# Alternating delta-rule pairs and state-space groups in the scan part of a hybrid decoder block

## The chip, the core and the metric

The kernel runs on one core of one Trainium2 chip. The metric is the device time of one execution in microseconds (us). The engines are TensorE (PE for products, PEld for the loads of the stationary operand), VectorE (DVE), ScalarE (ACT), GpSimd (POOL) and SyncE (SP), whose queue issues every DMA here. Each engine works its own list of instructions in order; a semaphore wait at the head of a list holds up all that stands behind it.

## The reference, cut to what matters

One decoder block on 512 tokens of width 1024, all in float32. A normed and modulated input `h` is projected by one wide matrix; two token mixers work on the parts, their outputs are projected up, gated, merged, projected out, and a squared-ReLU MLP follows.

```python
h = rmsnorm(x, norm_mix_pre) * (1 + sc1) + sh1
proj = h @ w_in                       # z_ssm, xbc, dt, qkv, z_gdn, b, a, gate_ssm, gate_gdn
xbc = silu(causal_conv4(xbc) + b)     # state-space branch: 32 heads in 8 groups, chunks of 128
  y_diag = (C B^T * decay) x ;  y_off = C state * exp(acum)
  state  = state * exp(a_last) + B^T (w_s x)
qkv = silu(causal_conv4(qkv))         # delta-rule branch: 16 value heads, 8 key/query heads
  (I + a_low) [u, w] = [v b, k b e^g]          # unit triangular solve
  v_new = u - w state ;  o = q e^g state + attn v_new
  state = state * exp(g_last) + k_dec^T v_new
merged = sigmoid(gate_ssm) * (y_ssm @ w_ssm_up) + sigmoid(gate_gdn) * (y_gdn @ w_gdn_up)
x = x + g1 * rmsnorm(merged @ w_out) ;  x = x + g2 * rmsnorm(relu(h2 @ w_mlp_up)**2 @ w_mlp_down)
```

## The kernel before, in words

Every dense product of two float32 matrices is made of three products of rounded parts (`mm3`, lines 147 to 150: high by high, low by high, high by low). Weights come in blocks of 128 by 1024 (`raw`), are split by ACT (high part) and DVE (low part), and three blocks of each kind are in flight. A block of 128 output channels costs 24 products of 512 columns.

The program has five stages. The **front** (0 to about 60 us of the trace) loads the tokens, builds the modulation and transposes `h` into `hT`. The **scan part** (to about 915 us) makes the dense products of `w_in` and runs the two mixers under them. Then come the **up-projections**, the **output projection**, and the **MLP**.

The scan part works on 16 items: items 0 to 7 are pairs of delta-rule heads (one key/query head, two value heads), items 8 to 15 are state-space groups of four heads. For each item there are:

- `dense_in(i)` (line 556): four blocks of channels, each followed by a four-tap convolution and Silu (`conv`). It writes the item's keys and queries into a ring of buffers `kq`.
- `dense_z(i)` (line 587): the gate z, products of 256 columns.
- a preparation, `gdn_prep` or `ssd_prep`. Both load a decay matrix by DMA (`decay`, line 690, tiles `dec` or `dc`; ACT then applies eight Relu pieces, line 697, and one Exp). `gdn_prep` forms the triangular matrix `bt` (line 768) from key products (PE, line 762) and starts `solve`.
- `solve` (line 799), delta-rule items alone: `bt` goes out to DRAM and back as `Nb` (line 808) so that all 32x32 blocks lie one row to a partition; 31 steps of two POOL operations (lines 817 and 819) invert them; the result goes to DRAM and back into a tile `U` (line 830).
- a scan. `gdn_scan` (line 834) widens the inverses from 32 to 128 (PE lines 850, 860, 863, 874, 882, with ACT writing `Z1` and `Z2` and DVE writing `T6` and `U` between), then runs the recurrence over four chunks: PE 897 (state by keys and queries), DVE 902, PE 918 (by `U`), DVE 923, PE 931 (state update), DVE 938. `ssd_scan` (line 1079) does the like with PE 1090, 1108 and 1111; POOL adds the skip term (line 1128).
- an end: norm, gate z, transposes (PE 998 or 1164) and a store of `y` to DRAM (`put_y`, line 704).

Eight further blocks of `w_in` (the branches' gates, `("g", g)`) are fillers inside the scan part; the other eight are made behind it (`proj_ch`, line 1225 on), where PE would otherwise wait for the reload of `y`.

The order of all this is not written out. `Weave` (line 33) is a planner that runs while the program is built: each piece of work is a generator that issues some instructions and yields an estimate of their duration (`PE(..)`, `A(n)`, `V(n)`, `G(n)`, or `("S", t)` for a latency such as a DMA), or a list with a mark to wait for. The planner keeps a clock per engine and always issues next the first stream in rank whose last result is expected by now. The dense stream has the last rank, so dense products fill the places where the planner thinks that no scan step is ready. The estimates thus set each engine's order of instructions, and nothing else; on the chip each instruction waits for its true operands. Rings such as `kq`, `dec`, `zs` limit how far a stream runs ahead; `pb` is a ring of three PSUM banks for the scan steps.

In the kernel before, the order of items is 0, 1, ..., 15: first all delta-rule pairs, then all state-space groups (`heads`, line 1171).

Of the kernel before, what the change touches and what calls it, by code (L numbers as in the profile page):

```python
# [10 lines left out]
F32 = mybir.dt.float32  # L11
# [103 lines left out]
def hybrid_block(ctx: ExitStack, tc: tile.TileContext, x, cols, drow, rows, w_ada, w_ch, w_z,  # L115
# [86 lines left out]
    NG = 8  # L202
# [6 lines left out]
    acap = {"bt": (3, 1), "zs": (3, 1), "kq": (3, 3), "vt": (2, 2), "dec": (4, 4)}  # L209
# [18 lines left out]
    def loads():  # L228
        """The first transfers, in the order of their use."""
# [147 lines left out]
    def early_ch(n):  # L377
# [3 lines left out]
        for k in range(KD):  # L381
# [3 lines left out]
            yield PE(0.64)  # L385
# [22 lines left out]
    Us = [sp.tile([P, 8, P], F32, name=f"U{i}", bufs=1) for i in range(2)]  # L408
# [8 lines left out]
    def chan_of(i):  # L417
        """Blocks of w_ch of a head pair or group, in the order of their use."""
# [5 lines left out]
    # the order of the dense products: heads' and groups' channels, their gates z, the branches' gates as fillers  # L424
    seq = [("in", 0), ("g", 0), ("g", 1), ("g", 2), ("in", 1), ("z", 0), ("in", 2), ("z", 1)]
    seq += [("g", g) for g in range(3, NG)]
    for i in range(3, 16):
        seq += [("in", i), ("z", i - 1)]
    seq.append(("z", 15))
    plan, adas = [], list(range(16))  # L430
    for kind, i in seq:
        blocks = [b for b in chan_of(i)] if kind == "in" else [64 + i] if kind == "g" else []
        plan += [("w", ("c", b), w_ch[1 + b]) for b in blocks if 1 + b not in early + later]
        if kind == "z":
            plan += [("w", ("z", i, h), w_z[2 * i + h]) for h in range(2)]
            for _ in range(2 if i > 14 else i > 0):
# [99 lines left out]
    def dense_ch(blk):  # L536
# [50 lines left out]
    def dense_z(i):  # L587
        if i > 2:
            yield [("end", i - 3)]
# [5 lines left out]
        for tp in range(2):  # L595
            bk, ps = yield from bank("ps")
            for th in range(2):
                ts = slice((2 * tp + th) * P, (2 * tp + th + 1) * P)
                for k in range(KD):
# [114 lines left out]
    def gdn_prep(hq):  # L714
# [12 lines left out]
        for j in range(2):  # L727
# [71 lines left out]
    def solve(hq, btu):  # L799
        """Inverses of the unit triangular 32x32 diagonal blocks: every fourth row of one on a partition."""  # L800
# [4 lines left out]
        yield ("S", 4.0)  # L805
# [7 lines left out]
        yield ("S", 4.0)  # L813
# [17 lines left out]
        yield ("S", 4.0)  # L831
        wv.mark(("U", hq))

    def gdn_scan(hq):
        if hq:
            yield [("scan", hq - 1)]
# [3 lines left out]
        U = Us[hq % 2]  # L840
# [6 lines left out]
        Z1 = sp.tile([P, 8, 32], F32, tag="Z1", name="Z1", bufs=1)  # L847
# [24 lines left out]
        Z2 = sp.tile([P, 8, 64], F32, tag="Z2", name="Z2", bufs=1)  # L872
# [15 lines left out]
        # the recurrence over chunks  # L888
# [62 lines left out]
    def gdn_out(hq, c, dec, kd, u2, o, qs, so, ku2, kqs):  # L951
# [17 lines left out]
        yield A(P, 2)  # L969
# [261 lines left out]
    # up-projections, gated merge  # L1231
# [32 lines left out]
    # output projection, residual, norm of the MLP's input  # L1264
# [254 lines left out]
```

## Time and profile before

| | |
|---|---|
| device time, median of 3 runs | 1552.59 us (1549.88 to 1553.95) |
| span of the profiled execution | 1540.2 us; its own device time is not listed |
| PE busy | 1488.7 us, 97% of the span |
| PEld, DVE, ACT, POOL busy | 1271.8, 879.4, 741.4, 373.7 us |
| mean granted TensorE clock | 0.977 of full speed |

The busy time of PE counts each product until its modelled end, and products overlap, so 97% hides a good deal: a product at half the clock is busy for longer. Reading it by stretches, with the granted clock beside it, tells more than the sum. The span leaves out what lies ahead of the first and behind the last instruction; the median is 12.4 us above it. A PE instruction in the kernel's order is two passes in the trace where its operands are plain float32, so counts differ by that factor.

### The profile page before, as it was taken

The page shows a single profiled execution, that of the slowest core. Times are in us where ns is not written, and L with a number is a line of the kernel's source. Part 1 is how long each engine was busy: PE and PEld are TensorE (multiplying, and loading weights), DVE is VectorE, ACT ScalarE, POOL GpSimd, SP SyncE. Part 2 cuts the span into 40 slices and gives each one's busy share as a digit, 9 for nine tenths or more (in the row PEclk, how much of TensorE's full clock was granted, in tenths as well). Part 3 has the DMA queues.
Part 4 walks back from the last instruction along what each step waited for, and adds up shares of the span by engine and source line. Part 5 has one row for each costly group of instructions (what it writes and reads, how often), then busy time and mean ns, then how long its engine had stood idle before and what let it go on. Part 6 is the DMA issues. An engine that isn't in the chain of part 4 may idle for free.

```text
span 1540.2 us, 22637 instructions
## 1 busy us (share of the span) xinstructions
PE 1488.7 (97%) x8520; PEld 1271.8 (83%) x8520; DVE 879.4 (57%) x1564; ACT 741.4 (48%) x1393; POOL 373.7 (24%) x715
## 2 busy tenths in 40 slices
PE   7999898999999889999999999999999999999998
PEld 7788787888878679888888978888887888888886
DVE  5776456665757666866766764252377524344344
ACT  5585335453455275775667735242345433232232
POOL 6203455163363370333332230000002000000002
PEclk9999899997999989999999999999999999999999
DMA  7434443343524523344433459553363322222221
GB/s 279 151 119 114 127 105 91 101 136 100 127 76 128 140 80 114 134 128 144 135 122 129 142 169 304 190 192 109 123 212 110 110 96 96 96 96 96 96 96 69
DMA packets 87069, 199.45 MB, mean 129 GB/s; under 512 B 32504, under 2 KB 33024, under 8 KB 86960
## 3 DMA queue, kind: packets, MB, share of 16 engines
q1 hardware_dynamic: 86960, 198.01, 40.5%
q8 instruction: 67, 1.10, 0.3%
q14 instruction: 42, 0.34, 0.1%
HBM read 181.10 MB, written 16.88 MB: 129 GB/s over the span
## 4 chain that ended last, share of the span: by engine, by line
PE 81%; DMA 7%; POOL 4%; DVE 4%; issue 2%; ACT 2%; SPq 1%; POOLq 0%; ACTq 0%; DVEq 0%
PE ps L148 15%; PE ps L150 15%; PE ps L149 15%; PE pl L150 8%; PE pl L148 8%; PE pl L149 8%; DMA dec<-acd 2%; PE pb L1108 2%; DMA Nb<-btd 2%; POOL Ub L819 1%; DMA dc<-acd 1%; POOL tm L817 1%; PE pb L897 1%; PE pb L918 1%; PE pb L954 1%
## 5 line engine op out<-in xcount | busy, mean ns | idle before, releaser
L148 PE MATMUL ps<-hT,whi 128*128 128x512 f32 x688 | 291.6, 424 | 0.1
L150 PE MATMUL ps<-hT,whi 128*128 128x512 f32 x688 | 272.5, 396 | 0.0
L149 PE MATMUL ps<-hT,wlo 128*128 128x512 f32 x688 | 271.8, 395 | 0.0
L144 DVE TENSOR_TENSOR wlo<-raw,whi 128x1024 fp32r<-128x1024 f32 x119 | 146.7, 1233 | 217.3 <-ACT whi L143 215.3
L143 ACT CAST whi<-raw 128x1024 fp32r<-128x1024 f32 x119 | 124.7, 1048 | 229.5 <-PE pl L149 62.7
L148 PE MATMUL ps<-whi,hT 128*128 128x256 f32 (+1 forms) x536 | 165.3, 308 | 0.0
L463 DVE TENSOR_TENSOR wlo<-raw,whi 128x1024 fp32r<-128x1024 f32 x98 | 124.7, 1274 | 55.9 <-ACT whi L461 55.5
L150 PE MATMUL ps<-wlo,hT 128*128 128x256 f32 (+1 forms) x536 | 155.7, 291 | 0.0
L149 PE MATMUL ps<-whi,hT 128*128 128x256 f32 (+1 forms) x536 | 155.4, 290 | 0.0
L150 PEld LDWEIGHTS ps<-hT,whi 128*128 128x128 f32 x688 | 131.0, 190 | 29.0
L148 PEld LDWEIGHTS ps<-hT,whi 128*128 128x128 f32 x688 | 131.4, 191 | 26.2 <-issue 1.1
L149 PEld LDWEIGHTS ps<-hT,wlo 128*128 128x128 f32 x688 | 131.6, 191 | 23.9 <-issue 0.4
L525 DVE SCALAR_TENSOR_TENSOR cv<-ps,col,cv 128x511 f32<-128x511 f32 (+1 forms) x180 | 132.8, 741 | 16.1 <-ACT cv L519 13.4
L461 ACT CAST whi<-raw 128x1024 fp32r<-128x1024 f32 x98 | 102.2, 1043 | 64.6 <-PE ps L150 40.9
L817 POOL TENSOR_TENSOR tm<-Ub,Nb 128x60 f32<-128x60 f32 (+24 forms) x248 | 81.3, 328 | 135.3 <-DMA Nb<-btd 117.4
L148 PEld LDWEIGHTS ps<-whi,hT 128*128 128x128 f32 x536 | 103.8, 194 | 2.1 <-issue 0.4
L149 PEld LDWEIGHTS ps<-whi,hT 128*128 128x128 f32 x536 | 103.8, 194 | 1.6
L150 PEld LDWEIGHTS ps<-wlo,hT 128*128 128x128 f32 x536 | 103.5, 193 | 1.2 <-DVE wlo L144 0.3
L819 POOL TENSOR_TENSOR Ub<-Ub,tm 128x60 f32<-128x60 f32 (+24 forms) x248 | 84.8, 342 | 19.4
L1410 POOL TENSOR_TENSOR ya<-ya,gate 128x512 f32<-128x512 f32 x4 | 5.9, 1474 | 324.8 <-ACT junk L1408 324.8
L148 PE MATMUL pl<-hT,whi 128*128 128x512 f32 (+1 forms) x184 | 66.7, 364 | 1.0 <-DVE hT L190 1.0
L149 PE MATMUL pl<-hT,wlo 128*128 128x512 f32 (+1 forms) x184 | 66.2, 363 | 0.4 <-DVE wlo L144 0.4
(496 smaller groups left out, 3138.1 us busy)
## 6 DMA issues: line engine op xcount, KB each, us to landing
raw<-in_w_ch SPq DMA_DIRECT2D x81, 512.0 KB
raw<-in_w_ada SPq DMA_DIRECT2D x48, 512.0 KB
raw<-in_w_z SPq DMA_DIRECT2D x32, 512.0 KB
raw<-in_w_up SPq DMA_DIRECT2D x32, 512.0 KB
raw<-in_w_mu SPq DMA_DIRECT2D x32, 512.0 KB
raw<-in_w_md SPq DMA_DIRECT2D x32, 512.0 KB
ydr<-y SPq DMA_DIRECT2D x32, 256.0 KB
dc<-acd SPq DMA_DIRECT2D x16, 512.0 KB
```

What stands on the lines that cost most here:

```text
L143: sc.copy(hi, raw)
L144: ve.tensor_sub(out=lo, in0=raw, in1=hi.bitcast(F32))
L148: pe.matmul(ps, lhsT=lhs[0], rhs=rhs[0], start=first, stop=False)
L149: pe.matmul(ps, lhsT=lhs[1], rhs=rhs[0], start=False, stop=False)
L150: pe.matmul(ps, lhsT=lhs[0], rhs=rhs[1], start=False, stop=last)
L461: sc.copy(hi, raw)
L463: ve.tensor_sub(out=lo, in0=raw, in1=hi.bitcast(F32))
L525: ve.scalar_tensor_tensor(out=t[:, s:], in0=ps[:, :T - s], scalar=col[:, o + k:o + k + 1], in1=t[:, s:], op0=MUL, op1=ADD)
L817: gp.tensor_tensor(out=t3, in0=Ub[:, 0:r, j:j + 1].to_broadcast([P, r, n]), in1=Nb[:, j:j + 1, j + 1:32].to_broadcast([P, r, n]), op=MUL)
L819: gp.tensor_tensor(out=Ub[:, 0:r, j + 1:32], in0=Ub[:, 0:r, j + 1:32], in1=t3, op=SUB)
L897: pe.matmul(psk[:, j * 256:(j + 1) * 256], lhsT=kq[:, c, j, :], rhs=S, start=True, stop=True)
L1108: pe.matmul(psy[:, h * 64:(h + 1) * 64], lhsT=M[h // 2][:, h % 2, c, :], rhs=xd[:, c, h, :], start=True, stop=True)
```

## The change

Three things change in the scan part, and all of them act through the planner.

1. **Order of items.** `ORDER` mixes pairs and groups: 0, 8, 1, 2, 9, 3, 10, 4, 11, 5, 12, 6, 7, 13, 14, 15. Scans, preparations, ends and dense work all follow it. `before(i, n)` is the item n places ahead in it.
2. **Buffers and fillers.** The ring `kq` gets four buffers for three (an item's dense work may begin once the scan four places ahead is done). Room for it comes from one `U` for two (a pair's inverses are loaded into `U` once the scan of the pair before has ended) and from `Z1` and `Z2` sharing a buffer. Five more gate blocks become fillers (13 for 8): two after the second gate z, three and five near the end; three are left to `proj_ch`.
3. **Estimates.** The durations that the planner uses are changed: ACT 0.27 + n/1330 us, DVE 0.19 + n/975, POOL 0.24 + n/500, three dense products 0.68 us (0.36 for 256 columns), decay load 8.0 us (4.0 before), `bt` to DRAM 5.5 (4.0), `Nb` 10.0 (4.0), store of the inverses 5.0 (2.3), load of `U` 5.0 (4.0).

```diff
+ORDER = (0, 8, 1, 2, 9, 3, 10, 4, 11, 5, 12, 6, 7, 13, 14, 15)
+FILL = {2: 2, 15: 3, 16: 5}
 def A(n, k=1, f="A"):
-    return f, k * (0.25 + n / 1400)
+    return f, k * (0.27 + n / 1330)
...
-    NG = 8
+    NG = 3 + sum(FILL.values())
-    spare = (("kq", 3), ("vt", 2))
+    spare = (("kq", 4), ("vt", 2))
...
-    Us = [sp.tile([P, 8, P], F32, name=f"U{i}", bufs=1) for i in range(2)]
+    Us = [sp.tile([P, 8, P], F32, name=f"U{i}", bufs=1) for i in range(1)]
...
-    seq += [("g", g) for g in range(3, NG)]
-    for i in range(3, 16):
-        seq += [("in", i), ("z", i - 1)]
-    seq.append(("z", 15))
+    line = ORDER
+    at = {i: n for n, i in enumerate(line)}
+    def before(i, n):
+        return line[at[i] - n] if at[i] >= n else None
+    seq, fill = [("in", line[0]), ("g", 0), ("g", 1), ("g", 2)], list(range(3, NG))
+    for n in range(1, 17):
+        seq += [("in", line[n])] if n < 16 else []
+        seq.append(("z", line[n - 1]))
+        seq += [("g", fill.pop(0)) for _ in range(FILL.get(n, 0))]
...
     def dense_in(i):
-        if i > 2:
-            yield [("scan", i - 3)]
+        if at[i] > 3:
+            yield [("scan", before(i, 4))]
...
     def decay(i, hd, dst, key):
-        yield ("S", 4.0)
+        yield ("S", 8.0)
...
     def solve(hq, btu):
-        if hq > 1:
-            yield [("scan", hq - 2)]
-        U = Us[hq % 2]
+        if hq:
+            yield [("scan", hq - 1)]
+        U = Us[0]
...
     def heads(one, two):
-        for i in range(8):
-            yield from one(i)
-        for i in range(8):
-            yield from two(i)
+        for i in line:
+            yield from one(i) if i < 8 else two(i - 8)
```

Line numbers in the changed kernel are higher by 2 in the front and by 10 or 11 in the scan part (PE line 897 becomes 908, 918 becomes 929, 931 becomes 942, 762 becomes 773, 850 becomes 861; ACT line 697 becomes 708; POOL line 817 becomes 828). How the order of instructions moves is shown at three places.

**PE, recurrence of a pair.** Before, pair 4, from its second state update (`u3`, L931) to the next product by the state (L897):

```order
L931 MATMUL pb_4467<-u3_4436,kt_3116 128x256
L148 MATMUL ps_4473<-whi_4072,hT_96 128x256
L149 MATMUL ps_4473<-whi_4072,hT_97 128x256
L150 MATMUL ps_4473<-wlo_4073,hT_96 128x256
L731 MATMUL pa_4479<-ident_69,kq_3957 128x128 x4
L897 MATMUL pb_4484<-S_4469,kq_2828 128x256 x2
L954 MATMUL pb_4495<-u2_4438,dec_3085 128x128 x2
```

Now, pair 5, from its second state update (L942) to the first product of the group behind it (L1102, `xw`):

```order
L942 MATMUL pb_6992<-u3_6979,kt_5503 128x256
L150 MATMUL ps_6880<-whi_6690,hT_110 128x256
L151 MATMUL ps_6880<-whi_6690,hT_111 128x256
L152 MATMUL ps_6880<-wlo_6691,hT_110 128x256
L908 MATMUL pb_7008<-S_6994,kq_4972 128x256 x2
L965 MATMUL pb_7017<-u2_6981,dec_5500 128x128 x2
L929 MATMUL pb_7024<-r_7011,U0_125 128x128 x2
L942 MATMUL pb_7040<-u3_7027,kt_5503 128x256
L908 MATMUL pb_7053<-S_7042,kq_4972 128x256 x2
L965 MATMUL pb_7062<-u2_7029,dec_5500 128x128 x2
L929 MATMUL pb_7066<-r_7056,U0_125 128x128 x2
L1102 MATMUL pb_7074<-xw_6481,bt__6166 128x256
```

Before, dense products stand between the steps; in the changed order pair 5 (and likewise pair 3) runs its third chunk and the start of the fourth with none between.

**ACT, a decay load beside a pair's scan.** Before, pair 6 (`Z`, L877 is its last widening step; L697 are the Relu pieces on `dc` of group 0; L908 empties a bank of the recurrence):

```order
L877 ACTIVATE Z_5511<-pb 64x512
L529 ACTIVATE vT<-cv 128x512
L697 ACTIVATE dc<-dc,tok_114 128x128 x4
L519 ACTIVATE cv<-ps,col 128x512
L697 ACTIVATE dc<-dc,tok_114 128x128 x2
L1023 COPY bt__5579<-pa 128x512
L697 ACTIVATE dc<-dc,tok_114 128x128 x4
L908 ACTIVATE qs<-pb,tok_115 128x128 x2
```

Now, pair 1 with the `dc` of group 1 (L708 are the Relu pieces, L919 empties the bank):

```order
L888 ACTIVATE Z_2921<-pb 64x512
L708 ACTIVATE dc<-dc,tok_114 128x128 x12
L472 CAST whi<-raw 128x1024
L532 ACTIVATE cv<-ps,col 128x512
L708 ACTIVATE dc<-dc,tok_114 128x128 x2
L711 ACT_TABLE_LOAD
L711 ACTIVATE dc<-dc 128x1024
L540 ACT_TABLE_LOAD
L540 ACTIVATE kq<-cv 128x4x128
L919 ACTIVATE qs<-pb,tok_115 128x128 x2
```

In both, Relu pieces on a tile that comes by DMA stand ahead of a step of the running recurrence.

**POOL, a solve.** Before, the start of pair 3's solve (`Ub`, `tm`, `Nb`):

```order
L986 TENSOR_TENSOR ro<-so,mhalf 128x8
L812 COPY Ub<-eye 128x256
L817 TENSOR_TENSOR tm<-Ub,Nb 128x31
L819 TENSOR_TENSOR Ub<-Ub,tm 128x31
L817 TENSOR_TENSOR tm<-Ub,Nb 128x30
L819 TENSOR_TENSOR Ub<-Ub,tm 128x30
```

Now, the start of the same solve (L828, L830), with the skip terms (L1140) and gate products (L1160) of group 1:

```order
L823 COPY Ub<-eye 128x256
L1140 TENSOR_TENSOR t__3976<-t__3976,xk 128x256
L1140 TENSOR_TENSOR t__4002<-t__4002,xk 128x256
L1140 TENSOR_TENSOR t__4022<-t__4022,xk 128x256
L828 TENSOR_TENSOR tm<-Ub,Nb 128x31
L830 TENSOR_TENSOR Ub<-Ub,tm 128x31
L828 TENSOR_TENSOR tm<-Ub,Nb 128x30
L830 TENSOR_TENSOR Ub<-Ub,tm 128x30
L828 TENSOR_TENSOR tm<-Ub,Nb 128x29
L830 TENSOR_TENSOR Ub<-Ub,tm 128x29
L1160 TENSOR_TENSOR xk<-xk,zs 128x256
L828 TENSOR_TENSOR tm<-Ub,Nb 128x28
```

Operations of a group now stand between the steps of a pair's solve, where before there were none.

More of the change, by code (lines that the diff above doesn't have):

```diff
@@ L96, in A @@
 def A(n, k=1, f="A"):
-    return f, k * (0.25 + n / 1400)
+    return f, k * (0.27 + n / 1330)
 def V(n, k=1):
-    return "V", k * ((0.11 if n < D else 0.07) + n / 960)
+    return "V", k * (0.19 + n / 975)
 def G(n, k=1):
-    return "G", k * (0.15 + n / 500)
+    return "G", k * (0.24 + n / 500)
 def PE(t):
@@ L205, in hybrid_block @@
     POOLW = (1, 3, 5)
-    spare = (("kq", 3), ("vt", 2))
+    spare = (("kq", 4), ("vt", 2))
     wspare = ("bt", "zs", "o")
     ahalf = ("bt", "zs", "kq", "vt", "kq", "vt", "kq", "bt", "zs", "kq", "dec", "dec", "dec", "dec", "vt", "kq")
-    acap = {"bt": (3, 1), "zs": (3, 1), "kq": (3, 3), "vt": (2, 2), "dec": (4, 4)}
+    acap = {"bt": (3, 1), "zs": (3, 1), "kq": (4, 4), "vt": (2, 2), "dec": (4, 4)}
     akeys = {}
@@ L384, in early_ch @@
             mm3(ps, (w[0][:, ks], w[1][:, ks]), hT[k], k == 0, k == KD - 1)
-            yield PE(0.64)
+            yield PE(0.68)
         wv.mark(("early", n))
@@ L422, in chan_of @@
         return 48 + g, 56 + g, 32 + 2 * g, 33 + 2 * g
-    seq = [("in", 0), ("g", 0), ("g", 1), ("g", 2), ("in", 1), ("z", 0), ("in", 2), ("z", 1)]
-    seq += [("g", g) for g in range(3, NG)]
-    for i in range(3, 16):
-        seq += [("in", i), ("z", i - 1)]
-    seq.append(("z", 15))
+    line = ORDER
[7 more added lines that the diff above has]
+        seq += [("g", fill.pop(0)) for _ in range(FILL.get(n, 0))]
+    assert not fill
     plan, adas = [], list(range(16))
@@ L435, in hybrid_block @@
             plan += [("w", ("z", i, h), w_z[2 * i + h]) for h in range(2)]
-            for _ in range(2 if i > 14 else i > 0):
+            for _ in range(2 if at[i] > 14 else at[i] > 0):
                 plan += [("a", (adas[0], hf), w_ada[2 * (8 + adas[0]) + hf]) for hf in range(2)]
@@ L550, in dense_ch @@
             mm3(ps, (w[0][:, ks], w[1][:, ks]), hT[k], k == 0, k == KD - 1)
-            yield PE(0.64)
+            yield PE(0.68)
         if 1 + blk not in later:
@@ L556, in dense_in @@
     def dense_in(i):
-        if i > 2:
-            yield [("scan", i - 3)]
-        first = sp.tile([P, NC, 2, P] if i < 8 else [P, 2, NC, P], F32, tag="kq", name="kq", bufs=3)
+        if at[i] > 3:
+            yield [("scan", before(i, 4))]
+        first = sp.tile([P, NC, 2, P] if i < 8 else [P, 2, NC, P], F32, tag="kq", name="kq", bufs=4)
         pair = []
@@ L587, in dense_z @@
     def dense_z(i):
-        if i > 2:
-            yield [("end", i - 3)]
+        if at[i] > 2:
+            yield [("end", before(i, 3))]
         zs = sp.tile([P, NC, 256], F32, tag="zs", name="zs", bufs=3)
@@ L735, in gdn_prep @@
                 if c == 1:
-                    yield A(P, 2)
+                    yield A(300, 2)
             if j == 0:
                 sc.copy(kt, ps.rearrange("p (a b) -> p a b", a=NC))
-            yield A(P, 2) + A(T, 1 - j)
+            yield A(300, 2) + A(T, 1 - j)
             wv.mark(bk)
@@ L804, in solve @@
             nc.sync.dma_start(out=btd[b].rearrange("u j i -> j u i"), in_=btu[bs, :, bs])
-        yield ("S", 4.0)
+        yield ("S", 5.5)
         turn_nb = yield from wv.slot("Nb", 1)
@@ L812, in solve @@
         gp.tensor_copy(out=Ub, in_=eye)
-        yield ("S", 4.0)
+        yield ("S", 10.0)
         for j in range(31):
@@ L830, in solve @@
             nc.sync.dma_start(out=U[bs, :, bs], in_=ubd[b].rearrange("u r i -> r u i"))
-        yield ("S", 4.0)
+        yield ("S", 5.0)
         wv.mark(("U", hq))
     def gdn_scan(hq):
-        if hq:
-            yield [("scan", hq - 1)]
+        if at[hq]:
+            yield [("scan", before(hq, 1))]
         yield [("U", hq)]
@@ L839, in gdn_scan @@
         kq, kt, vt, dec, bt, bb, bw, rq, keys, kd = pre.pop(hq)
-        U = Us[hq % 2]
+        U = Us[0]
         btu = bt.rearrange("p c j i -> p (c j) i")
@@ L846, in gdn_scan @@
         bk, ps = yield from bank("pb")
-        Z1 = sp.tile([P, 8, 32], F32, tag="Z1", name="Z1", bufs=1)
+        Z1 = sp.tile([P, 8, 32], F32, tag="Z", name="Z1", bufs=1)
         for b in (0, 64):
@@ L871, in gdn_scan @@
         bk, ps = yield from bank("pb")
-        Z2 = sp.tile([P, 8, 64], F32, tag="Z2", name="Z2", bufs=1)
+        Z2 = sp.tile([P, 8, 64], F32, tag="Z", name="Z2", bufs=1)
         for q in range(8):
@@ L1080, in ssd_scan @@
         i = 8 + g
-        yield [("scan", i - 1)]
+        if at[i]:
+            yield [("scan", before(i, 1))]
         yield [("prep", i)]
```

6 lines of the change are left out of this document (3 added, 3 removed).

## The prediction

> **What bounds the kernel now.** I read the 40 slices first, then windows of 50 us, then PE's waits, then what the named releasers themselves waited for.
>
> ```profile
> span 1540.2 us, 22637 instructions
> PEclk9999899997999989999999999999999999999999
> ```
>
> The granted clock falls early, in slices 4 to 15, that is in the stretch of the delta-rule pairs. The windows (columns: length; busy PE, PEld, DVE, ACT, POOL; granted clock; DMA share; GB/s) give it sizes:
>
> ```profile
> 150.00:200.00 50.00, 44.97 (x321) 38.74 (x320) 23.60 (x50) 19.18 (x43) 26.58 (x74) 0.86 0.39 108
> 200.00:250.00 50.00, 45.29 (x311) 37.49 (x310) 27.90 (x70) 22.60 (x58) 24.11 (x73) 0.97 0.42 114
> 350.00:400.00 50.00, 47.64 (x332) 43.13 (x331) 29.41 (x71) 22.98 (x64) 25.62 (x67) 0.80 0.32 96
> 450.00:500.00 50.00, 46.10 (x358) 39.95 (x357) 34.62 (x82) 24.71 (x68) 18.16 (x52) 0.97 0.40 114
> 500.00:550.00 50.00, 38.77 (x287) 32.57 (x286) 30.03 (x61) 19.03 (x41) 21.60 (x61) 0.90 0.45 114
> 700.00:750.00 50.00, 50.00 (x322) 44.79 (x322) 33.97 (x54) 32.36 (x58) 17.68 (x16) 1.00 0.41 128
> 900.00:950.00 50.00, 47.14 (x212) 38.46 (x212) 28.41 (x42) 28.04 (x46) 7.63 (x8) 0.97 0.76 249
> ```
>
> In the groups' stretch (700 to 750 stands for it) PE is full at full clock: nothing is to be had there. In the five windows of the pairs PE idles 5.0 + 4.7 + 2.4 + 3.9 + 11.2 = 27.2 us, and its busy time is stretched by (1 - clock) x busy = 6.3 + 1.4 + 9.5 + 1.4 + 3.9 = 22.5 us. Together 49.7 us are lost, 1.83 us for each idle one. At the end of the scan part it is 2.9 + 1.4 = 4.3 us. So **54 us** is all that a better order of the scan part can win. What ends the idle time:
>
> ```profile
> PE pb L897 <- DVE S L941: 9.9, 1, 9.9
> PE pb L850 <- DVE T L842: 6.7, 4, 2.4
> PE pb L897 <- ACT y L707: 4.7, 1, 4.7
> PE pb L882 <- ACT Z L877: 2.7, 1, 2.7
> ...
> ACT dc L697 <- DMA dc<-acd: 30.2, 13, 11.7
> ACT dec L697 <- DMA dec<-acd: 24.2, 5, 10.2
> ...
> POOL tm L817 <- DMA Nb<-btd: 117.4, 8, 20.3
> ```
>
> There are two causes. ACT stands in order behind Relu pieces (L697) whose decay tile has not landed, and so Z, y or the emptying of a bank comes late: 9.9 + 4.7 + 2.7 us. And the inverses of a pair (L842 reads U) come late: 6.7 us. In the groups' stretch the same ACT waits cost PE next to nothing, since dense products stand behind.
>
> **Decay loads.** The chain of waits shows the time from issue to landing at the three stalls:
>
> ```profile
> 174.77 12.44 DMA dec<-acd
> 225.73 12.80 DMA dec<-acd
> 526.00 15.47 DMA dc<-acd
> ```
>
> The planner assumed 4 us. Counting the PE work that stands in the order between the load's issue and the first Relu, these three loads had 7.5, 4.2 and 2.5 us of cover, and PE idled 2.7, 4.7 and 9.9: landing less cover less idle leaves a slack of 2.2, 3.9 and 3.1, mean 3.1. The change assumes 8 us. In its order three loads still fall into a pair's scan: pair 1 (cover 10.0, two loads behind an Nb, as the 15.5 one was), pair 6 (11.4, the same), pair 7 (7.3, one load, 12.5). Idle: 15.5 - 10.0 - 3.1 = 2.4, then 1.0 and 2.1, together **5.5 us**, between 0 (if ACT runs behind the plan) and 14.8 (no slack). The other loads stand outside pairs' scans, where ACT's waits cost PE nothing.
>
> **Solves.** From a pair's last key product (L762) to its first widening product (L850), where the latter waited:
>
> ```profile
> 120.06 1.02 PE L762 MATMUL pa<-kq 128*128 128x256 f32 x4
> 174.47 1.75 PE L850 MATMUL pb<-T,bt 32*32 32x32 f32 x32 [2.37 <-DVE T L842]
> 291.03 1.02 PE L762 MATMUL pa<-kq 128*128 128x256 f32 x4
> 352.66 1.80 PE L850 MATMUL pb<-T,bt 32*32 32x32 f32 x32 [2.36 <-DVE T L842]
> 396.41 1.02 PE L762 MATMUL pa<-kq 128*128 128x256 f32 x4
> 461.68 0.69 PE L850 MATMUL pb<-T,bt 32*32 32x32 f32 x16 [0.74 <-DVE T L842]
> ```
>
> So a solve needs 54.4, 61.6 and 65.3 us, mean 60.4. What covers it is the PE work between. Its price at full and at half clock:
>
> ```profile
> 183.44 0.39 PE L149 MATMUL ps<-hT,wlo 128*128 128x512 f32 x1
> 183.67 0.39 PE L150 MATMUL ps<-hT,whi 128*128 128x512 f32 x1
> ...
> 175.00:182.00 7.00, 7.00 (x43) 5.21 (x41) 2.02 (x5) 0.75 (x2) 0.00 (x0) 0.51 0.80 216
> ```
>
> Products of 512 columns start 0.23 us apart, those of 256 half of that (0.12). In the order before, the thinnest solve has 123 and 60 of them and 107 small instructions: 28.3 + 7.2 + 17.3 = 52.8 us; all eight have 53 to 61, about or under the need. In the changed order the thinnest (pair 6) has 147, 99 and 92: 33.8 + 11.9 + 21.4 = 67.1; the eight are 70.9, 82.9, 72.1, 76.3, 70.7, 81.4, 67.1 and 72.8. The need grows too, as the groups' POOL work now stands inside the solves:
>
> ```profile
> L1148 POOL TENSOR_TENSOR xk<-xk,zs 128x256 f32<-128x256 f32 x32 | 32.8, 1041 | 23.3 <-ACT zs L614 23.3
> L1073 POOL TENSOR_TENSOR xk<-xk,dsk 128x512 f32<-128x512 f32 x16 | 19.1, 1195 | 0.3 <-ACT xk L1068 0.3
> ```
>
> Up to four of the first and two of the second, two of its twin L1071, and one or two small ones: 6 to 10 us a solve by the order, mean 8.3, where the three solves above had 2.7. Need: 60.4 + 5.6 = 66.0, at most 71. At 66 nothing is late, at 71 it is 0.1 + 0.3 + 3.9 = 4.3 us; I take **1 us**.
>
> **Pairs 3 and 5.** Their third chunk runs without dense work, since the dense stream has run ahead to the limit of the kq ring. The chain needs:
>
> ```profile
> 599.15 1.03 PE L897 MATMUL pb<-S,kq 128*128 128x256 f32 x4
> 600.22 0.61 DVE L902 SCALAR_TENSOR_TENSOR r<-pb,neg,vt 128x128 f32<-128x128 f32 x2 [0.27 <-PE pb L897]
> 601.18 0.61 PE L918 MATMUL pb<-r,U 128*128 128x128 f32 x4
> 601.83 0.42 DVE L923 TENSOR_TENSOR u<-pb,bw 128x256 f32<-128x256 f32 x1 [0.28 <-PE pb L918]
> 603.06 0.60 PE L931 MATMUL pb<-u,kt 128*128 128x256 f32 x2
> 603.70 0.61 DVE L938 SCALAR_TENSOR_TENSOR S<-S,elast,pb 128x128 f32<-128x128 f32 x2 [0.72 <-PE pb L931]
> ```
>
> From one PE start to the end of the DVE step behind it: 1.7, 1.1 and 1.25 us. PE's own work in these places is 1.2, 0.4 and 0.25 (0.6 with the last dense triple). PE idles 0.65 + 0.5 + 0.7 + 1.0 + 0.5 = 3.3 us in each pair, **6.6 us** in all, which are new.
>
> **The rest** I cost at nothing, and name the cover. Single U: pairs 2 and 7 follow another pair, and their load waits for its scan; the order puts 25 us of PE work between, against 5 us for such a load by the planner's new figure; uncovered it would be 2 x 5 us idle. Five gate blocks move, 24 x 0.23 = 5.5 us each, the same work elsewhere. Behind the scan three blocks are left, 16.5 us, to cover the reload of y:
>
> ```profile
> 914.20 1.07 PE pb L1164 x5
> ...
> 923.11 2.64 DVE L1221 TENSOR_TENSOR yl<-yr,yl 128x512 fp32r<-128x512 f32 x4 [1.35 <-ACT yl L1220]
> ```
>
> The first four tiles were ready 925.75 - 914.20 = 11.6 us after the last transposes, 5 us ahead of need; PE then takes 48 x 0.23 = 11 us per four tiles. In front, the loads keep their order.
>
> **Sum.** Idle 5.5 + 1 + 6.6 = 13.1 us, at the 1.83 of before 24 us. Gain 54 - 24 = 30 us: span 1510, and, the 12.4 us around it unchanged, 1552.6 - 30 = **1522 us**.
>
> The 1.83 can be disputed: L850 at 174.47 waited 2.37 us, and in the next 7 us the clock was 0.51. The Trainium skill (TensorE: Matmul & The Clock Gate, What's actually happening) has the clock halved after an idle window of about 3.4 us. Here a shorter gap was enough, so the trace does not agree in the size; by the page the short gaps of pairs 3 and 5 would cost their 6.6 us alone, and the sum would be 1517.
>
> **Rivals.** (a) *All is covered*: ACT runs behind the plan and the small gaps cost themselves alone. 54 less 6.6: 1505. For it speaks the groups' stretch, full in spite of ACT's waits; against it the bare chunk of pairs 3 and 5. Chance 0.20. (b) *No change*: solves need 74 us; then 3.1 + 1.9 + 3.3 + 6.9 + 1.2 = 16.4 us of idle at five pairs, with the 12.1 above 28.5 x 1.83 = 52 us: 1551. The need would have to be 3 us over the highest that I derive. Chance 0.07. (c) *Slower*: POOL becomes the bound of the solves. L817 waits in order for Nb, and the skip terms and gate products of the groups stand among the steps; each also collides with DVE.
>
> ```profile
> L817 POOL TENSOR_TENSOR tm<-Ub,Nb x248: 201/291/1318, 137.9 to 565.4; 128x60 f32<-128x60 f32 x12, 128x54 f32<-128x54 f32 x8, 128x66 f32<-128x66 f32 x8, 128x28 f32<-128x28 f32 x8
> L1043 DVE TENSOR_TENSOR dc<-dc,cb 128x1024 f32<-128x1024 f32 x16 | 19.8, 1251 | 1.7 <-POOL cb L1036 1.2 <-ACT dc L700 0.5
> ```
>
> A step takes 0.29 us as a rule and up to 1.3, the length of a large DVE product, and a group brings two of these. It decides from a need of 75 us; at 78 the eight lack 7.1 + 5.9 + 1.7 + 7.3 + 10.9 + 5.2 = 38 us, with 12.1 above 50 x 1.83 = 92, less 54: 38 us slower, 1590. Against it: such products are few, 2.5 us a solve. Chance 0.08. The Trainium skill (SBUF — State Buffer, Who interferes with whom) states that a VectorE instruction with two SBUF inputs holds up a GpSimd one that reads SBUF; the longest L817 agrees, and it bears on (c) alone.
>
> **Numbers.** Forecast (1510 to 1540) 0.55, (a) 0.20, a half-way case with the ACT term at 14.8 and the solve term at 4.3 us (25.7 x 1.83 = 47 of the 54 us, 1545) 0.10, (b) 0.07, (c) 0.08. A measurement of this kernel tells about 0.3% (4.7 us) from no change. Faster 0.85, same 0.07, slower 0.08. Range 1500 to 1549, which leaves out (c), part of (b), and the deepest part of (a).
>
> **What would show it.** Right: granted clock 1.00 in most windows from 150 to 900; no wait of the widening product for DVE's T6 over 1 us; ACT's waits for dec and dc well under 54 us; gaps of at most 1 us in the recurrences of pairs 3 and 5, and a clock that dips there. Wrong: the widening products waiting at several pairs, with POOL busy without a gap ahead of them; skip terms of a group ending PE's waits; SP held at a load of U; a gap at the start of the up-projections.

## The result

The changed kernel takes 1514.43 us (median of 4 runs, 1514.09 to 1519.71) beside 1551.89 us (1549.88 to 1553.95, 4 runs) for the kernel before: ratio 0.9773, interval 0.9747 to 0.9799, so 37.5 us or 2.3% faster. A second set of runs, on another chip, gave 1515.69 us (4 runs) and again 0.9773 (0.9744 to 0.9802). The forecast was 1522, in a range of 1500 to 1549.

The profiled execution of the changed kernel took 1519.71 us, the slowest of its four. First its span and the 40 slices of the clock:

```profile
span 1518.0 us, 22650 instructions
PEclk8999999999999999999999999999999999999999
```

The row that fell to 7 and 8 in the pairs' stretch now stands at 9, that is at 90% or more, throughout. By windows (columns as in the prediction; the last window is the whole scan part from 150 us on):

```profile
150.00:200.00 50.00, 50.00 (x366) 43.13 (x364) 28.60 (x49) 30.02 (x57) 27.20 (x56) 1.00 0.40 126
350.00:400.00 50.00, 47.76 (x300) 42.64 (x300) 34.72 (x85) 17.94 (x44) 10.00 (x18) 0.93 0.32 99
450.00:500.00 50.00, 46.45 (x299) 41.03 (x299) 33.96 (x85) 18.03 (x43) 9.44 (x20) 0.93 0.31 98
650.00:700.00 50.00, 46.03 (x306) 39.84 (x303) 33.49 (x84) 19.92 (x54) 13.78 (x24) 0.93 0.27 78
700.00:750.00 50.00, 50.00 (x371) 42.93 (x369) 30.93 (x58) 25.63 (x51) 25.96 (x66) 1.00 0.57 156
850.00:900.00 50.00, 44.81 (x269) 38.30 (x268) 30.56 (x60) 24.61 (x51) 16.71 (x19) 0.93 0.47 153
150.00:915.00 765.00, 747.17 (x5077) 652.56 (x5076) 517.89 (x1048) 426.02 (x931) 322.84 (x629) 0.98 0.40 123
```

The same long window of the kernel before:

```profile
150.00:915.00 765.00, 734.20 (x4988) 643.60 (x4986) 503.56 (x1042) 423.61 (x915) 303.24 (x616) 0.96 0.40 120
```

TensorE idled 765 - 734.20 = 30.8 us of the scan part before and 17.8 us now, and the clock rose from 0.96 to 0.98. What is left sits in four windows: pair 2 (350 to 400), pair 3 (450 to 500), pair 5 (650 to 700), and the last group (850 to 900). The waits of the changed kernel, PE's own first and then those of the engines that had made PE late before:

```profile
PE pb L942 <- DVE u L934: 4.6, 2, 2.8
PE ps L150 <- ACT whi L472: 4.6, 1, 4.6
PE ps L151 <- DVE wlo L474: 2.5, 3, 1.5
PE pb L908 <- DVE S L949: 2.5, 2, 1.7
PE pb L965 <- DVE u L937: 2.5, 2, 2.2
...
ACT dc L708 <- DMA dc<-acd: 9.6, 5, 3.5
...
POOL tm L828 <- DMA Nb<-btd: 21.5, 4, 7.7
...
DVE T L853 <- DMA U<-ubd: 3.1, 2, 1.7
```

No widening product (L861) waits for T6 any more, and no `Z` or `y` stands behind a decay load: ScalarE's waits for `dc` and `dec` went from 30.2 + 24.2 to 9.6 us (all `dc`), and POOL's for `Nb` from 117.4 to 21.5. The last row is the solves: VectorE stood at its first transpose of `U` (L842 before, L853 now) at two pairs for 3.1 us, where it had stood at five:

```profile
DVE T L842 <- DMA U<-ubd: 16.4, 5, 5.1
```

### The profile page after: what moved, and what is told of

Read it like the earlier page. It is cut to its first block, busy times and chain, and to the rows that moved or that the text cites. A ratio compares the mean times of both kernels' runs of the same rounds, so it can differ in the third digit from the quotient of the medians.

```text
span 1518.0 us, 22650 instructions
## 1 busy us (share of the span) xinstructions
PE 1481.2 (98%) x8528; PEld 1264.1 (83%) x8528; DVE 889.9 (59%) x1564; ACT 739.2 (49%) x1392; POOL 386.3 (25%) x714
## 5 line engine op out<-in xcount | busy, mean ns | idle before, releaser
L150 PE MATMUL ps<-hT,whi 128*128 128x512 f32 x688 | 287.2, 417 | 5.4 <-ACT whi L472 4.6
L152 PE MATMUL ps<-hT,whi 128*128 128x512 f32 x688 | 270.2, 393 | 0.0
L474 DVE TENSOR_TENSOR wlo<-raw,whi 128x1024 fp32r<-128x1024 f32 x103 | 130.9, 1272 | 81.7 <-ACT whi L472 81.5
L150 PE MATMUL ps<-whi,hT 128*128 128x256 f32 (+1 forms) x536 | 164.6, 307 | 0.0
L150 PEld LDWEIGHTS ps<-hT,whi 128*128 128x128 f32 x688 | 130.3, 189 | 31.4 <-ACT whi L472 4.8
L150 PEld LDWEIGHTS ps<-whi,hT 128*128 128x128 f32 x536 | 102.1, 191 | 3.5 <-issue 0.9
L830 POOL TENSOR_TENSOR Ub<-Ub,tm 128x60 f32<-128x60 f32 (+24 forms) x248 | 99.9, 403 | 19.4
L151 PEld LDWEIGHTS ps<-whi,hT 128*128 128x128 f32 x536 | 102.2, 191 | 2.2
L828 POOL TENSOR_TENSOR tm<-Ub,Nb 128x60 f32<-128x60 f32 (+24 forms) x248 | 84.5, 341 | 36.7 <-DMA Nb<-btd 21.5
L150 PE MATMUL pl<-hT,whi 128*128 128x512 f32 (+1 forms) x184 | 66.6, 363 | 1.0 <-DVE hT L192 1.0
```

What stands on the lines that cost most here:

```text
L150: pe.matmul(ps, lhsT=lhs[0], rhs=rhs[0], start=first, stop=False)
L151: pe.matmul(ps, lhsT=lhs[1], rhs=rhs[0], start=False, stop=False)
L152: pe.matmul(ps, lhsT=lhs[0], rhs=rhs[1], start=False, stop=last)
L474: ve.tensor_sub(out=lo, in0=raw, in1=hi.bitcast(F32))
L828: gp.tensor_tensor(out=t3, in0=Ub[:, 0:r, j:j + 1].to_broadcast([P, r, n]), in1=Nb[:, j:j + 1, j + 1:32].to_broadcast([P, r, n]), op=MUL)
L830: gp.tensor_tensor(out=Ub[:, 0:r, j + 1:32], in0=Ub[:, 0:r, j + 1:32], in1=t3, op=SUB)
```

## The experiments

Every ratio is to the kernel before on the same chip. The table is the summary; idle is 765 us less PE's busy time in the window 150 to 915 of each profile. The window is fixed, while the scan part ends between 876 us (e7) and 965 us (e3); beyond 915 us e3 has two more waits, of 2.87 and 2.75 us.

| kernel | items | durations | kq, U | late or moved fillers | us | ratio (interval) | idle, us | span, us |
|---|---|---|---|---|---|---|---|---|
| before | pairs first | old | 3, 2 | no | 1548 to 1552 | 1 | 30.8 | 1540.2 |
| e2 | pairs first | new | 3, 2 | no | 1539.5 | 0.9949 (0.9931-0.9967) | 30.9 | 1542.6 |
| e6 | pairs first | old | 4, 1 | late | 1547.4 | 0.9984 (0.9960-1.0007) | 32.3 | 1546.3 |
| e7 | pairs first | new | 4, 1 | no | 1503.7 | 0.9695 (0.9669-0.9721) | 9.9 | 1504.1 |
| e4 | pairs first | new | 4, 1 | late | 1506.1 | 0.9739 (0.9720-0.9758) | 14.1 | 1504.9 |
| e8 | pairs first | new | 4, 1 | moved | 1496.9 | 0.9659 (0.9625-0.9693) | 8.9 | 1494.5 |
| e10 | pairs first | new | 4, 1 | moved, none last | **1491.0** | 0.9626 (0.9585-0.9668) | 5.5 | 1489.7 |
| e3 | alternating | old | 4, 1 | late | 1582.2 | 1.0201 (1.0157-1.0245) | 46.2 | 1590.5 |
| the change, e5 | alternating | new | 4, 1 | late | 1515.7 | 0.9773 (0.9744-0.9802) | 17.2 | 1513.0 |
| e9 | alternating | new | 4, 1 | moved | 1506.9 | 0.9731 (0.9693-0.9768) | 14.8 | 1504.3 |
| e11 | alternating | new but one (solve) | 4, 1 | late | 1536.3 | 0.9913 (0.9885-0.9941) | 33.3 | 1535.3 |
| e12 | alternating | new but one (decay) | 4, 1 | late | 1519.8 | 0.9810 (0.9771-0.9850) | 22.1 | 1517.6 |

### What lies around the span: e1 and e5

> The kernel before, once more with a profile. Its first profile has a span of 1540.2 us although its timed runs are 1550 to 1554, while the changed kernel's device time is 1.7 us above its own span. Theory 'spread': executions of the kernel before differ by some 10 us among themselves, and its device time too is span plus 1.7; then this profile shows a span from 1540 to 1552 with more idle time of PE in the stretch of the pairs when it is longer. Rival 'offset': something of about 12 us lies outside the span in this kernel alone; then the span is about 1540 again with a device time of about 1552.

The kernel before, once more: 1542.22 us with a span of 1540.5. So a device time is its span and 1.7 us, and the theory of a constant 12.4 us around the span falls: the profiled execution of before simply took some 1542 us, while the timed ones of all sets lay between 1541 and 1557. With the same span as the first profile this one has 35.3 us of idle in the scan part, not 30.8, but less time at a lowered clock (0.97 over the scan part, not 0.96): the idle time alone does not fix the span.

> The change itself once more, beside the next three on one chip. Every theory: 1506 to 1520 us, ratio 0.973 to 0.981. If its profiled span is 1518 again while the timed runs give less, the profiled execution is slower by itself; if span plus 1.7 us lies among the timed runs, executions of this kernel merely differ by some 6 us.

The second profile of the change has a span of 1513.0 where the first had 1518.0. (The expectations of e7 and e8 count the fillers loosely: the change has thirteen, three in front and ten by its table, eight of these late; with the three in front e7 has 8, e8 14, e9 13 and e10 12.) The two profiles compare as follows, the first above, the second below:

```profile
0.00:50.00 50.00, 42.38 (x261) 38.47 (x261) 32.06 (x53) 28.12 (x44) 26.00 (x39) 0.90 0.66 245
```

```profile
0.00:50.00 50.00, 43.20 (x275) 38.56 (x276) 35.12 (x59) 30.59 (x48) 27.41 (x42) 0.97 0.74 272
150.00:915.00 765.00, 747.78 (x5084) 653.45 (x5083) 517.91 (x1048) 426.98 (x932) 322.95 (x626) 0.99 0.41 125
```

In the first 50 us the granted clock was 0.90 in one execution and 0.97 in the other, with 14 products fewer begun. From 150 to 915 both have 17 to 18 us of idle, at the same places. Part of the difference arises there all the same, through the clock. In both, the step at pair 2 waits 2.25 us for `u` (L965, at 374.85 and at 372.17 us); the stretch at half clock that goes with it lasts 6.8 us in the first execution and 3.4 us in the second:

```profile
374.20:381.00 6.80, 6.15 (x19) 5.23 (x20) 4.59 (x14) 1.87 (x7) 2.22 (x2) 0.50 0.65 176
```

```profile
371.80:375.20 3.40, 3.04 (x11) 2.88 (x12) 2.54 (x6) 1.59 (x5) 1.10 (x1) 0.50 0.77 191
375.20:378.60 3.40, 3.40 (x16) 2.81 (x15) 1.98 (x10) 0.00 (x0) 1.42 (x1) 1.00 0.54 163
```

### Which part of the change wins: e2, e3, e4, e6, e7

e2 is the kernel before with the new durations alone:

```diff
 def V(n, k=1):
-    return "V", k * ((0.11 if n < D else 0.07) + n / 960)
+    return "V", k * (0.19 + n / 975)
...
     def decay(i, hd, dst, key):
-        yield ("S", 4.0)
+        yield ("S", 8.0)
...
     def solve(hq, btu):
-        yield ("S", 4.0)
+        yield ("S", 10.0)
```

> The kernel before with the new estimates alone: items in the order 0 to 15, three kq buffers, two U, eight fillers. By its order the solves have 65 to 78 us of PE work as cover (53 to 61 before), but the recurrences of five pairs run bare, as the dense stream stands at the limit of the kq ring: 18.9 us of chain without cover by the prediction's working (7.7 in the changed kernel). Theory 'cover' (the loss is what cover is missing, at about 2 us for each idle one): 38 us from the bare chains, some 15 from ACT's waits and the rest: about 1535 us, between 1525 and 1545. Rival 'estimates' (they alone bring the gain): 1514. Rival 'alternation' (mixing the items alone brings it): 1552.

1539.49 us, 0.5% faster. The solves are covered now (no wait for T6 in its list), but the idle time is as large as before, 30.9 us. PE waits for other things:

```profile
PE pb L882 <- ACT Z L877: 10.3, 2, 6.3
PE pb L897 <- DVE S L938: 6.9, 6, 2.2
PE pb L931 <- DVE u L923: 5.2, 8, 1.6
```

The first row is the prediction's decay load: ScalarE had stood 7.04 us at a `dec` and 8.08 us at a `dc` just ahead of the two `Z` that PE waits for:

```profile
357.12 1.86 ACT L697 ACTIVATE dec<-dec,tok 128x128 f32<-128x128 f32 x6 [7.04 <-DMA dec<-acd]
530.16 0.69 ACT L697 ACTIVATE dc<-dc,tok 128x128 f32<-128x128 f32 x2 [8.08 <-DMA dc<-acd]
```

The two last rows of PE's waits are the recurrence run bare: with solves started earlier, the dense stream reaches the limit of three `kq` buffers before the recurrence is through. By the order 18.9 us of chain stand in five pairs with nothing beside them.

e6 is the other half: pairs first, four `kq` buffers, one `U`, the change's fillers, and the old durations (the change with `ORDER = tuple(range(16))` and the lines above turned back).

> Pairs first and groups after them, with the four key buffers, the single U and the later fillers of the change, but the old durations in the planner. Theory 'cover' (a stall is the traced need less the PE work that the order leaves for it): the covers of the solves are 54 to 61 us, as before the change (53 to 61), those of the decay loads 1.8 us in the mean, as before (1.7): 1540 to 1560 us, ratio 0.993 to 1.005. Rival 'buffer' (the fourth key buffer lets dense products run ahead, whatever the durations say): 1505 to 1525 us.

1547.43 us, not told apart from before. The covers of the solves are as short as they were, and VectorE waits for `U` at seven pairs:

```profile
DVE T L853 <- DMA U<-ubd: 20.6, 7, 8.1
...
PE pb L861 <- DVE T L853: 10.1, 6, 4.9
```

So neither the durations nor the buffer does much by itself. e4 has both, with pairs first:

```diff
-ORDER = (0, 8, 1, 2, 9, 3, 10, 4, 11, 5, 12, 6, 7, 13, 14, 15)
+ORDER = tuple(range(16))
```

> The changed kernel with the items in the order 0 to 15 again; estimates, kq ring, single U and fillers as changed. By its order all solves have 69 to 75 us of cover and 1.6 us of chain are bare. Theory 'cover': no slower than the changed kernel, 1500 to 1515, although nothing alternates. Rival 'alternation': 1540 or more, with PE idle in the stretch of the pairs as before. Rival 'single U' (pairs that follow each other wait for U's load): widening products wait for DVE's T6 at most pairs, 5 us each, about 1550.

1506.05 us: the whole gain of the change is there without its first part. What remains of the change's gains if the late fillers go as well shows e7 (`FILL = {2: 5}`, the eight blocks of before at their places).

> Pairs first, new durations, four key buffers, single U, but eight filler blocks at the places of before instead of eleven with eight of them late. Theory 'cover': solves 68 to 77 us, bare chain 0.6 us, decay loads 6.7 us in the mean, all as in the linear order with late fillers: 1500 to 1510 us, ratio 0.970 to 0.977. Rival 'fillers' (late fillers feed TensorE while the pairs and groups end): 1520 to 1530 us.

1503.67 us, so the late fillers bring nothing either. From 0.9949 for the new durations with three buffers to 0.9695 with four, 2.6%, is what the fourth buffer (with the single `U` that makes room for it) is worth once the solves start early; with the old durations (e6, which has the late fillers too) nothing can be told from it, 0.2% with an interval that includes none. The single `U` and the shared buffer of `Z1` and `Z2` were not tried apart from it.

e3 is the change with the old durations alone put back.

> The changed kernel with the old estimates: mixed order, four kq buffers, one U, thirteen fillers. By its order the solves have 52 to 69 us of cover, the decay loads 2.0 us on average (1.7 before, 7.4 in the changed kernel), and no chain runs bare. Theory 'cover': the late inverses and ACT's waits of the kernel before come back in part: 1530 to 1550. Rival 'alternation': 1514 to 1520. Rival 'estimates': 1552.

1582.15 us, 2% slower than before the change, outside of what any of the theories had. Its waits, and two of the rows:

```profile
PE pb L861 <- DVE T L853: 22.0, 6, 7.1
...
DVE T L853 <- DMA U<-ubd: 31.2, 6, 8.3
```

```profile
181.35 1.84 PE L861 MATMUL pb<-T,bt 32*32 32x32 f32 x32 [7.06 <-DVE T L853]
...
669.74 2.02 PE L861 MATMUL pb<-T,bt 32*32 32x32 f32 x32 [4.82 <-DVE T L853]
```

Here the solves can be timed, since they are waited for: from the last key product to the widening product it takes 61.3, 66.1, 74.1, 73.6, 77.6 and 68.7 us at the six pairs that wait, mean 70.2, where three pairs of the kernel before gave 60.4 (a fourth that waited, pair 6, took 64.9). In e6, with the same buffers but pairs first, the seven for which VectorE waits took 64.7 in the mean. The covers by the order are 52 to 69 us, mean 61, against 57 before. So alternating items made the solves 5 to 10 us longer and lengthened their cover by 4. The traces show where in part: from a solve's first POOL step to the end of its last it takes 34.2 us in e3 and 30.5 in e6 (means of eight pairs). Of the 3.7 us more, other POOL operations among the steps are 2.2 (6.2 against 4.0), and the steps themselves 1.8 (23.2 against 21.4). No run took the group operations out alone.

### The bare recurrences: e9, and the queue of VectorE

```diff
-FILL = {2: 2, 15: 3, 16: 5}
+FILL = {2: 2, 6: 1, 8: 1, 12: 1, 15: 2, 16: 3}
```

> The change with its alternating order, and its eleven - here ten - filler blocks at other steps: 2 after the second, 1 each after the sixth, eighth and twelfth, 2 and 3 at the end. Theory 'cover': the recurrences of pairs 2, 3 and 5, where 7.7 us of chain had no product of another stream beside it, are down to 1.8 us: 5.9 us less idle, at 1.83 us each 11 us: 1499 to 1510 us, ratio 0.966 to 0.973, and no gap of 1 us or more left in the recurrences of pairs 3 and 5. Rival 'queue' (those gaps come from the place of the recurrence's steps in VectorE's queue, not from missing products): 1512 to 1520 us.

1506.91 us, ratio 0.9731: by the ratios about 7 us better than the change, where 11 were expected, with intervals that overlap. The gaps of pairs 2, 3 and 5, 9.8 us in the changed kernel, are gone; one of 0.80 us at pair 4 is the largest that remains of this kind:

```profile
569.98 0.68 PE L965 MATMUL pb<-u,dec 128*128 128x128 f32 x4 [0.80 <-DVE u L937]
```

The idle time fell by 2.4 to 3 us only, because waits elsewhere grew: PE now stands 3.42 us at the last transposes (L1176) and 2.11 us at a pair's (L1009), where the changed kernel had none and 0.22.

The rival (the place in VectorE's queue) had half of it, too. The changed kernel at pair 3, PE first, then VectorE:

```profile
469.34 0.75 PE L929 MATMUL pb<-r,U 128*128 128x128 f32 x4
472.85 0.95 PE L942 MATMUL pb<-u,kt 128*128 128x256 f32 x2 [2.76 <-DVE u L934]
474.59 2.05 PE L908 MATMUL pb<-S,kq 128*128 128x256 f32 x4 [0.79 <-DVE S L949]
```

```profile
471.23 1.23 DVE L474 TENSOR_TENSOR wlo<-raw,whi 128x1024 fp32r<-128x1024 f32 x1 [1.02 <-ACT whi L472]
472.37 0.42 DVE L934 TENSOR_TENSOR u<-pb,bw 128x256 f32<-128x256 f32 x1
```

The step `u` that PE waits for stood in VectorE's queue behind a weight split (L474), which itself waited 1.02 us for ScalarE. A dense product beside the chain hides this, and that is what e9 put there; without one, it costs 2.76 us and not the 0.5 of the chain alone.

### The weight split near 865 us: e8 and e10

In the changed kernel the largest single gap stands at the last group. ScalarE's rows and the product behind them:

```profile
868.69 0.60 ACT L625 ACTIVATE zs<-ps 128x512 f32<-128x512 f32 x1 [1.48 <-PE ps L152]
869.30 1.28 ACT L711 ACT_TABLE_LOAD   x1
870.60 1.06 ACT L711 ACTIVATE dc<-dc 128x1024 f32<-128x1024 f32 x1
871.56 0.68 ACT L708 ACTIVATE dc<-dc,tok 128x128 f32<-128x128 f32 x2
872.15 1.03 ACT L472 CAST whi<-raw 128x1024 fp32r<-128x1024 f32 x1
```

```profile
873.23 0.79 PE L150 MATMUL ps<-hT,whi 128*128 128x512 f32 x1 [4.58 <-ACT whi L472]
```

ScalarE's order puts the split of the next weight block behind a gate `zs` that needs the product just ended, and between the two stand 2.9 us of work on a decay tile (`dc`: a table load, the Exp, two Relu pieces): no TensorE work is left to cover gate, decay work and split. Counted in the order, this cover is 0.0 us in the change, e4, e8 and e9, and 0.7 and 1.4 us in e11 and e12; all six have fillers after the last gate. e8 moves fillers (`{2: 2, 7: 2, 8: 1, 15: 2, 16: 4}`, pairs first), e10 has none after the last gate (`{2: 2, 7: 2, 8: 1, 14: 2, 15: 2}`).

> As the linear order with the new durations, with eleven fillers spread as 2 after the third step, 2 after the seventh, 1 after the eighth, 2 and 4 at the end. Theory 'cover': solves 69 to 75 us, no bare chain at all (1.6 us in the linear order, which at 1.83 us each is 3 us), decay loads 7.4 us: 1498 to 1508 us, ratio 0.969 to 0.975, not slower than the linear order. Rival 'tail' (what is left after 850 us is a weight split that ScalarE issues late at the last group, and fillers taken from there lengthen it): 1508 to 1515 us.

1496.85 us, 1 us below the range of the theory of covers; the stall at the split stays, 3.13 + 1.75 us at 867 us.

> The linear order with moved fillers, but none after the last step: 2 after the second, 2 after the seventh, 1 after the eighth, 2 each after the fourteenth and fifteenth. In the orders with fillers after the last step one weight split near 865 us is issued on ScalarE with no product of TensorE left ahead of its first use (0.0 us by the order), here every split has over 3 us but one of 3.0. Theory 'cover': the 4.9 us of idle at that split go: 1486 to 1495 us, ratio 0.958 to 0.965. Rival 'tail' (the last groups wait for something else by then): 1495 to 1505 us.

1490.97 us, as expected, and the lowest of all kernels: 0.9626 of the time before, some 23 us below the change by the ratios. The interval overlaps that of e8; that the stall is gone is seen in the profile, and the scan part is all but full:

```profile
150.00:915.00 765.00, 759.50 (x5170) 664.06 (x5170) 518.91 (x1055) 444.92 (x945) 303.65 (x616) 1.00 0.43 134
```

### One duration back at a time: e11 and e12

e11 sets the estimate ahead of the solve's steps back from 10 to 4 us, e12 that of a decay load from 8 to 4 us, both in the changed kernel.

> The change with one duration of its planner back at the old value: 4 us instead of 10 between the send of a solve's blocks and the use of the answer. By the order the solves have 62 to 78 us of cover (67 to 83 in the change), short of a need of 66 us by 0.8, 4.2 and 2.5 us in pairs 0, 2 and 7; the bare chain comes out at 2.1 instead of 7.7 us. Theory 'cover' with a need of 66 us: TensorE waits some 7 us for T6, which is worth +14 us against -10 us of the chain: 1512 to 1524 us. Rival 'need 60' (the solve is faster than 62 us when fewer loads run beside it): no wait for T6, 1500 to 1511 us.

1536.34 us, slower than both theories said. PE waits for T6 in it, as a need of 66 us has it, but only 4.3 us (7 were expected) of its 33.3 us of idle are that. The rest are waits that were in no count of mine:

```profile
PE ps L151 <- DVE wlo L474: 6.5, 5, 2.6
PE pb L1009 <- DVE o L1003: 4.8, 3, 2.2
PE ps L150 <- ACT whi L472: 4.5, 2, 4.0
PE pb L861 <- DVE T L853: 4.3, 2, 2.8
```

One changed duration moves every stream behind it, so this run does not measure the solve's cover alone. The rival (need 60, no wait) falls; the size of the rest stays unexplained but for its places.

> The change with the planner's duration of a decay load back at 4 us instead of 8. By the order a decay load has 3.4 us of cover in the mean instead of 7.4, while the loads took 4.6 to 12.2 us, 7.0 in the median, in the change; the bare chain is 2.7 instead of 7.7 us. Theory 'late ScalarE' (the prediction's step: ScalarE stands at the load and the recurrence behind it is late): four loads inside pairs, short by 4 us each, 16 us at 1.83, less 9 us for the chain: 1525 to 1545 us. Rival 'slack' (ScalarE waits for its loads more than 30 us instead of 10, and has the idle time for it): 1502 to 1514 us.

1519.82 us, between both theories, and by the intervals not told apart from the change (0.9810 against 0.9773). ScalarE's waits for the loads:

```profile
ACT dc L708 <- DMA dc<-acd: 21.2, 11, 5.5
ACT dec L708 <- DMA dec<-acd: 6.8, 3, 4.5
```

They went up from 9.6 to 28.0 us, and PE's idle time from 17.2 to 22.1. Sixteen us of stalled recurrences, as the theory of the late ScalarE had it, did not come: here these waits are mostly absorbed, and the new gaps of PE stand elsewhere (2.43 us at a widening product that waits for T6, 2.65 + 1.39 us at a weight split). In e2 they were not: two loads cost PE 10.3 us.

## Why the prediction was right, and where not

**The bound, 54 us.** It was somewhat too low: e10, with 5.5 us of idle left in the scan part, is 57.9 us below the kernel before by the medians (1548.84 on its chip). By the spans of the profiles it is 50.5; the difference is that of the point on the span, below.

**1.83 us for each idle us.** A line through span and idle time of the 13 profiles in the table (two of the change among them) has a slope of 2.23 us, and meets 1474 us at no idle; nine profiles lie within 4 us of it, e3 and e11 13 off, to either side. The steep end is e3, whose scan part runs past the window; without e3, and with e1, the slope is 1.84. The forecast's rate was good, but as a mean of two things. The clock record of each trace has stretches at half clock of 3.4, 6.8, 10.2 us and so on up to 20.5, all but each execution's last a multiple of 3.4. An idle us costs itself, and the stretches around it cost half of their length. Span less all of PE's idle time and less half of the time at half clock comes to 1459 to 1470 us in all 14 profiles, e3 and e11 among them.

A rate of one for the short gaps of pairs 3 and 5, with 1517 us, falls: the windows with gaps of 1.7 to 2.8 us in pairs 2, 3 and 5 have a clock of 0.93. (That rate came from the Trainium skill, TensorE: Matmul & The Clock Gate, What's actually happening, where the clock is halved after an idle window of about 3.4 us; these gaps are shorter, so the trace does not agree.) In the two profiles of the change these 7.5 us of gaps went with 13.7 and 10.2 us at half clock, and so cost 14.4 and 12.6 us: 1.9 and 1.7 us for each idle one.

**12.4 us around the span** was wrong: it is 1.7 (e1). The profiled execution of before was one of its fastest. The spans of the change's two profiles are 22 and 27 us below that of before, where the forecast had 30; the medians differ by 37.5. So the forecast's span, 1510, was 3 to 8 us too low, and its 12.4 us around it 10.7 too high. The two errors cancel in part, and that 1522 came within 8 us of 1514 owes something to luck. The kernel before takes 6 to 10 us more in the median of its runs than in its two profiles. No profile shows where, but the clock listed with each timed run goes with it: 0.972 to 0.976 at 1554 to 1557 us, 0.979 to 0.981 at 1541 to 1544.

**Decay loads, 5.5 us of idle:** none was seen at those places. Of 54 us of ScalarE's waits 9.6 are left, in five waits, and the longest is 3.5. The term was a landing time of 12.5 to 15.5 us, taken from the three worst loads of before; in the changed kernel the `dc` loads landed in 4.6 to 12.2 us, 7.0 in the median, and the `dec` loads in 4.5 to 6.0. The mechanism itself stands: e2 has it twice, for 10.3 us of PE's time, while in e12 28 us of such waits cost little.

**Solves, 1 us of idle:** none on PE, but the margin was thinner than the sum said. VectorE still waited for `U` at two pairs, 3.1 us, and there the solve can be timed in the changed kernel itself. From the last key product to VectorE's first read of `U` it took 76.0 us at pair 4 and 73.0 at pair 7. So the need of 66, at most 71, was too low for alternating items; e3 has 61 to 78, mean 70.2. The share of POOL was sized well: other operations among a solve's steps take 8.5 us in the mean, 2.7 before, where 8.3 was forecast. The steps themselves went from 20.8 to 23.1 us, which the sum left out and rival (c) named. What saved the two thinnest covers was luck: PE's own idle time and lowered clock, which stretch a cover. Pairs 4 and 6, 70.7 and 67.1 us by count, had 77.0 and 74.1 us from the last key product to the widening, because the gaps of pairs 3 and 5 lie in these stretches. Rival (c), POOL making the solves longer, did happen in its first half, the longer need; the new durations had made room for it. With the old ones it decides (e3, 1582 us, near the 1590 of that rival).

**Pairs 3 and 5, 6.6 us of idle:** 2.76 + 0.79 and 0.44 + 1.83 + 1.70, that is 7.5 us. The size was right, and the clock dips there (0.93); e9 took it away by putting products there. The make-up was not: not steps of the chain at half a us to 1 us each (the sign named for it, gaps of at most 1 us, did not come), but three long gaps, and at each of these a weight split stands ahead of the step in VectorE's queue.

**What was not foreseen:** a gap of the same kind in pair 2 (2.25 us, `u` behind L474), and the weight split at the last group, 4.58 + 0.61 us in the profiled execution. Both are places where a split, at the last group with decay work ahead of it, stands in an order with nothing to cover it. They make up 7.4 us of idle, somewhat more than the 5.5 that the decay loads were wrongly given.

**The single U, the gate blocks, the reload of y** cost nothing, as forecast: e4, e7 and e10 have one `U` and no wait for it above 1.9 us, and PE had no gap at the start of the up-projections.

**What the gain was made of** the prediction left open, since it read the final order. The runs settle it: the durations and the fourth buffer together, 2.6 to 3.1% with pairs first; neither alone more than 0.5%; and alternating items not at all: with the new durations e5 stands 0.3% behind e4, with intervals that overlap, and with the old ones e3 2.2% behind e6, with intervals far apart.

## What to carry to other kernels

Where a planner sets the order, count in that order how much work of the bounding engine stands between a request and its use, for every kind of request (loads, solves, weight splits, the steps of a recurrence), and compare it with the traced time of each; a gap shows up where the cover is short, and it costs about twice its length here. A longer lead needs a buffer in which the work that fills it can be put, so change durations and buffers together: each alone did 0.5% or less. Measure an interleaving with and without the rest of a change before it is kept.

## What the runs showed of the chip that had not been expected

- Two executions of the changed kernel have spans of 1518.0 and 1513.0 us, with the idle time of the scan part the same to 0.6 us. They are 2.7 us apart by 223 us (L965 at 223.14 and 220.46) and 6.4 at the last group (L150 at 873.23 and 866.80): the front, with a clock of 0.90 or 0.97 in its first 50 us, makes part of it, and stretches at half clock of 6.8 or 3.4 us beside the same gaps in pairs 2 and 3 make most of the rest.
- Kernels with more idle time vary more from run to run: before 1541 to 1557 us, e3 1570 to 1592, e11 1527 to 1543, but e10 1489.8 to 1491.7. That the same gap can cost a shorter or a longer stretch at half clock fits this; that it is the whole reason is not shown.
- Of 765 us in the scan part, 25.3 us less idle (30.8 to 5.5) went with a span shorter by 50.5 us, while the granted clock of that window went from 0.96 to 1.00.
